# Score products of two attentions over all 128 rows of the array, and a small-tile path to memory for one attention's output

## The chip, the cores and the metric

The kernel runs on one core of one Trainium2 chip. The metric is the device time of one execution, from the first instruction to the last, in microseconds. TensorE (PE) multiplies, VectorE (DVE) and ScalarE (ACT) read the products out of PSUM, GpSimd (POOL) works between tiles in SBUF, and the queue of SyncE (SP) issues all transfers to and from memory.

## The reference

Two decoder layers run one after another on 1024 tokens of 1024 features. In each, one input projection is split into four token mixers, whose outputs go through one output projection, a layer norm, a SwiGLU feed-forward part and a second layer norm. The change lies in two of the mixers, which are both attentions with four heads:

```python
# mixer B: latent attention; keys and queries have 64 plain and 32 rotary features
q = rms_norm(c_q) @ w_uq;  kv = rms_norm(c_kv) @ w_ukv
q = concat([q[..., :64], rope(q[..., 64:])]);  k = concat([k_nope, rope(k_r)])   # k_r is shared by the heads
o = softmax(q @ k.T * 96 ** -0.5, causal) @ v
# mixer C: dilated attention; three branches with masks of their own, merged by their softmax sums
o = sum_r w_r * softmax(q @ k.T * 0.125, mask_r) @ v          # q, k rotated, 64 features
# after the mixers
x = layer_norm(alpha * x + concat([y_a, y_b, y_c, y_d]) @ w_out)
```

The three branches of mixer C have one score matrix, and the kernel folds their masks into one additive mask (`maskC`), so that both mixers run through the same routine.

## The kernel before

**Products in split form.** A float32 operand is held as a high part and a low part in float32r, and a product is taken as high x high + high x low + low x high. In the score product of one head (64 features) the stationary tile `q1[hh]` holds the head's high query part twice, on rows 0 to 63 and on rows 64 to 127, and the moving tile `kst[hh]` holds the high key part on one half of the rows and the low key part on the other. One product over 128 rows so gives high x high and high x low. The third part, low query x high key, is a product over 64 rows alone: `qlo[half]` against `kst[hh][half]`, where `half` is the 64 rows of the head (scores, line 793). Mixer B adds the rotary part as a third product, over 96 rows: `QR` has the 32 rotary features as (high, high, low), `R` as (high, low, high).

**Attention.** `attn` goes through 64 rows in each layer: four groups of 16 (mixer C heads 0 and 1, C heads 2 and 3, B heads 0 and 1, B heads 2 and 3), and in a group 2 heads x 8 query tiles of 128 tokens, a short row and a long one in turn. Row i has (i + 1) x 128 keys in pieces of at most 512. So a group has 24 score pieces, a layer 96, the kernel 192: 96 of mixer C with two products each, 96 of mixer B with three. A row goes through this chain:

- PE: the score products of a piece into a PSUM tile `sc` (L119 is the helper that issues them).
- DVE: scale, mask and running minimum of the negated scores into `P` (L798); for rows of two pieces one more instruction takes the minimum of the two (L802).
- ACT: the exponential in place with the row sum (L805). DVE: the reciprocal (L807). POOL: `P` times the reciprocal (L808).
- PE: 128x128 transposes of `P` (L825). ACT and DVE: split into `PH` and `PL` (L138, L141).
- PE: products with the values (L846). ACT: two copies of 64x256 out of PSUM into `tmp` (L853, L854). POOL: their sum (L855) into the output tile, `Yc` for mixer C and `Yb` for mixer B.

**What sets the order.** On PE the order is written by hand: scores run 3 rows ahead of the transposes, and these 2 rows ahead of the values (`AHEADS`, `VLAG`). Between them stand jobs in small pieces: the last projection tiles of mixer C (`zc`), the transposes of its queries and keys (`ptc`), and, within the second group, the projections of mixer B (`prb`, `pvb`, `ptr`, `pkb`, `pqb`). On the other engines a scheduler orders the instructions, and each engine then takes them strictly one after another. Tiles come from pools of a fixed number of buffers (A, B, E, w, t2); a tile gets a buffer when an earlier one is released.

**Around it.** `put_q` fills `q1` and `qlo` from PSUM, for half of the tokens at a time. The projections of mixer B's queries have the same form as the scores: the features 128 to 191 of the latent stand on 64 rows as high parts and on the other 64 as low parts (`Q2`); the product with the low weights is over 64 rows (`wq[1][0:64]`, lines 1005 and 1052). At the end of the second group, `end1` writes both `Yc` tiles to memory (`spill`), from where the output projection reads them back (`yr`).

Of the kernel before, what the change touches and what calls it, by code (L numbers as in the profile page):

```python
# [7 lines left out]
F32 = mybir.dt.float32  # L8
# [7 lines left out]
D = 1024  # L16
# [31 lines left out]
class Split:  # L48
    """the parts of a float32 array, each a tile of its own: [:, 0, columns] the high part, [:, 1, columns] the low one"""
# [8 lines left out]
class Net:  # L58
# [84 lines left out]
    # ---------------------------------------------------------------- consts  # L143
# [22 lines left out]
    def warm(self, n):  # L166
        """products that nothing reads, while the first operands come in: the tensor engine is slow when it starts"""
# [6 lines left out]
    def rope_tables(self):  # L174
# [27 lines left out]
        # cos(r) = sin(pi/2 - |r|)  # L202
# [7 lines left out]
    def rope(self, out, src, nh, hf, cs, sn, add_eng=None):  # L210
        """src [128, nh, 2*hf] PSUM; cs/sn [128, 2*hf]; out [128, nh, 2*hf] or with a leading copy dim."""
# [6 lines left out]
        if out is None:  # L218
            return a, b
        for o in out:  # L220
            (add_eng or nc.vector).tensor_tensor(out=o, in0=a, in1=b, op=ALU.add)
# [10 lines left out]
    def first_pair(self, T):  # L232
        """the first two k tiles of weights and tokens, one after the other, to start the products early"""
# [15 lines left out]
    def dense_tok(self, out, T, tt, W, n, c0, nn, ks=range(KD)):  # L249
        """out[128 tokens, nn] += x @ W[:, c0:c0+nn]; W units hold two k tiles of n columns."""  # L250
# [11 lines left out]
    def dense_jobs(self, name, T, tt, W, n, c0, nn, evac, step=6):  # L262
        """dense_tok as a list of steps of a few products each"""
# [24 lines left out]
    # ------------------------------------------------------------- mixer A  # L288
    def mix_a(self, l, T):
# [24 lines left out]
        # keep w[s, t] where t - s >= 0  # L314
# [28 lines left out]
        for h in range(2):  # L343
# [4 lines left out]
            if wide:  # L348
                # all token tiles of the half together, as the operands come in
# [34 lines left out]
    # ------------------------------------------------------------- mixer D  # L384
    def mix_d(self, l, T):
# [312 lines left out]
    # ------------------------------------------------------------- projections of B and C  # L698
    def z_b(self, l, T):
# [5 lines left out]
        krt = self.uw("kr", F32, "E")  # L705
        kr, junk = krt[:, 0:768].rearrange("p (t n) -> p t n", t=NT), krt[:, 768:960]
        for t in range(NT):
# [17 lines left out]
            outs = [kr[:, t, a * 32:(a + 1) * 32].unsqueeze(1) for a in range(3)]  # L725
            self.rope(outs, src, 1, 16, self.cs2[:, t, 0:64:2], self.sn2[:, t, 0:64:2])
        return ckv, cq1, cq2, kr

    def z_c(self, l, T):
        """both head pairs; the last four token tiles of the second pair are left as jobs"""  # L730
        nc, io = self.nc, self.io
        out, jobs = [], []
        for g in range(2):
# [3 lines left out]
            def evac(pz, t, q=q, k=k, v=v):  # L737
                nc.scalar.copy(v[:, t, :], pz[:, 256:384])
                src = pz[:, 0:256].rearrange("p (h j) -> p h j", j=64)
                a, b = self.rope(None, src, 4, 32, self.cs2[:, t, :], self.sn2[:, t, :])  # L740
# [12 lines left out]
    # ------------------------------------------------------------- attention  # L753
    def qk_tiles(self, pool):
        f = lambda n: self.u(n, F32R, pool)
        return [f("kst") for _ in range(2)], [f("q1") for _ in range(2)], self.u("qlo", F32R, "A")
# [8 lines left out]
    def put_q(self, pq, q1, qlo, cols):  # L765
# [925 lines left out]
```

## Time and profile before

| | us |
|---|---|
| median of 3 runs (2571.95 to 2581.69) | 2574.62 |
| span of the profiled execution | 2581.1 |
| PE busy in it | 2483.1 (96%) |
| DVE busy | 1682.5 (65%) |
| POOL busy | 1291.1 (50%) |
| ACT busy | 1039.9 (40%) |
| attention of the first layer, first score product to the output projection in steady run | 284.4 to 497.3 |
| attention of the second layer | 1573.9 to 1783.5 |

The profiled execution stands 6.5 us above the median, at the upper end of the three runs. The busy time of PE adds up the records of its products; they overlap, and a product that waits inside the array still counts as busy. How densely PE works is therefore read from the time between the starts of two products that follow each other, and not from its busy time. The granted clock (PEclk) is a share of full speed: 1.00 is 2.4 GHz, 0.50 is 1.2 GHz, and a value between them is a stretch with both.

### The profile page before, as it was taken

To read this page: it belongs to the slowest core of one execution; us is meant where nothing else is said; L and a number is where in the kernel's file an instruction comes from. 1 tells how busy PE (TensorE), PEld (TensorE's weight loads), DVE (VectorE), ACT (ScalarE), POOL (GpSimd) and SP (SyncE) were. 2 spreads that over 40 slices of the span, in tenths; PEclk is the share of its full clock that TensorE was granted. 3 is DMA by queue.
4 is the path that set the end of the run, shared out by engine and by line. 5 is a ranking of instruction groups with operands and counts; after the bars stand their busy time and mean duration, and the time that the engine had idled before them with its cause. 6 is when DMAs were issued, how large, how long until landed. Compare 5 with 4: busy or idle time off the path is not lost.

```text
span 2581.1 us, 33291 instructions
## 1 busy us (share of the span) xinstructions
PE 2483.1 (96%) x11884; PEld 2007.8 (78%) x11884; DVE 1682.5 (65%) x3132; ACT 1039.9 (40%) x2102; POOL 1291.1 (50%) x1116
## 2 busy tenths in 40 slices
PE   9999999998999999999899999999989999999997
PEld 9779767786888888778697797667868888887675
DVE  7643587458555455999966435775686554559998
ACT  6322577524323323433343225685343333234331
POOL 2014324566545454879520143245665544448795
PEclk9999999899999999999999999999999999999998
DMA  4111001331221223612131110014212222235121
GB/s 162 47 33 46 13 1 66 126 111 49 90 90 66 89 92 117 225 66 82 70 94 43 33 46 13 1 57 144 102 50 98 82 74 90 82 136 207 67 81 65
DMA packets 60822, 206.94 MB, mean 80 GB/s; under 512 B 8098, under 2 KB 8418, under 8 KB 60658
## 3 DMA queue, kind: packets, MB, share of 16 engines
q1 hardware_dynamic: 60658, 204.82, 22.8%
q8 instruction: 95, 1.56, 0.3%
q14 instruction: 69, 0.57, 0.1%
HBM read 158.62 MB, written 46.17 MB: 79 GB/s over the span
## 4 chain that ended last, share of the span: by engine, by line
PE 74%; DVE 15%; POOL 4%; issue 3%; ACT 3%; DMA 2%; POOLq 0%; DVEq 0%; SPq 0%; ACTq 0%
PE gu L119 30%; PE dn L119 5%; PE zc L119 5%; PE sc L119 5%; PE zvo L567 4%; PE po L119 4%; PE zdq L519 4%; PE za L119 3%; PE pv L846 3%; PE zb L119 2%; PE pt L825 2%; POOL dc L1254 2%; DVE ma L1467 1%; PE dl L119 1%; DMA hr<-hs 1%
## 5 line engine op out<-in xcount | busy, mean ns | idle before, releaser
L119 PE MATMUL gu<-T,fc 128*128 128x512 f32 x2640 | 636.0, 397 | 19.3 <-POOL T L1329 6.4
L119 PEld LDWEIGHTS gu<-T,fc 128*128 128x128 f32 x2640 | 499.6, 190 | 142.2 <-POOL T L1329 8.8
L1254 POOL TENSOR_TENSOR fc<-fw,fc 128x512 fp32r<-128x512 f32 x264 | 366.4, 1390 | 367.5 <-ACT fc L1253 363.5
L119 PE MATMUL dn<-dc,dc 128*128 128x512 f32 x1512 | 365.3, 402 | 21.6 <-DVE md L1518 5.4
L119 PEld LDWEIGHTS dn<-dc,dc 128*128 128x128 f32 x1512 | 287.5, 192 | 99.2 <-DVE ma L1518 8.5
L1253 ACT CAST fc<-fw 128x512 fp32r<-128x512 f32 x264 | 162.6, 620 | 373.3 <-PE gu L119 234.8
L1378 DVE TENSOR_TENSOR Ra<-Ra,gu 128x512 f32<-128x512 f32 x172 | 117.3, 684 | 225.1 <-PE gu L119 221.9
L119 PE MATMUL gu<-B,fc 128*128 128x512 f32 x1056 | 260.9, 396 | 0.0
L119 PEld LDWEIGHTS gu<-B,fc 128*128 128x128 f32 x1056 | 197.9, 188 | 47.2
L808 POOL TENSOR_SCALAR P<-P,rs 128x256 f32<-128x256 f32 (+7 forms) x128 | 95.9, 755 | 203.3 <-DVE rs L807 162.7
L1254 POOL TENSOR_TENSOR dc<-hr,dc 128x512 fp32r<-128x512 f32 x104 | 165.0, 1595 | 49.2 <-ACT dc L1253 47.6
L119 PE MATMUL po<-wh,yT 128*128 128x512 f32 x512 | 162.1, 396 | 0.0
L132 POOL TENSOR_TENSOR wl<-raw,wh 128x768 fp32r<-128x768 f32 (+2 forms) x40 | 81.6, 2046 | 116.2 <-ACT wh L127 114.9
L119 PE MATMUL zc<-wh,xT 128*128 128x384 f32 x512 | 134.8, 340 | 0.0
L1253 ACT CAST dc<-hr 128x512 fp32r<-128x512 f32 x104 | 64.6, 621 | 154.9 <-PE dn L119 50.4
L119 PEld LDWEIGHTS po<-wh,yT 128*128 128x128 f32 x512 | 95.7, 188 | 22.1
L825 PE MATMUL pt<-ident,P 128*128 128x128 f32 x576 | 94.8, 291 | 15.3 <-DVE PL L141 10.0
L1254 POOL TENSOR_TENSOR dc<-dr,dc 128x512 fp32r<-128x512 f32 x68 | 108.9, 1601 | 0.0
L805 ACT ACTIVATE P<-P,mn 128x256 f32<-128x256 f32 (+7 forms) x128 | 99.2, 776 | 15.7 <-DVE mn L802 11.9
L119 PE MATMUL dl<-wl,hl 128*128 128x512 f32 x384 | 96.0, 407 | 9.8 <-DVE mc L1518 8.4
L141 DVE TENSOR_TENSOR PL<-pt,PH 128x512 fp32r<-128x512 f32 (+3 forms) x176 | 95.2, 557 | 12.0 <-ACT PH L138 11.1
L119 PE MATMUL po<-wl,yT 128*128 128x512 f32 x256 | 100.3, 394 | 0.0
(380 smaller groups left out, 5190.2 us busy)
## 6 DMA issues: line engine op xcount, KB each, us to landing
fw<-in_wGU SPq DMA_DIRECT2D x88, 512.0 KB, 3.8
dr<-in_wD SPq DMA_DIRECT2D x44, 512.0 KB, 5.6
hr<-hs SPq DMA_DIRECT2D x44, 512.0 KB, 6.3
hs<-Ra SPq DMA_DIRECT2D x22, 512.0 KB, 2.6
hs<-Rb SPq DMA_DIRECT2D x22, 512.0 KB, 2.9
raw<-in_wO SPq DMA_DIRECT2D x16, 512.0 KB, 3.6
x<-x SPq DMA_DIRECT2D x16, 512.0 KB, 2.6
raw<-in_wC SPq DMA_DIRECT2D x16, 384.0 KB, 3.0
```

What stands on the lines that cost most here:

```text
L119: self.nc.tensor.matmul(out, lhsT=a, rhs=b, start=first and j == 0, stop=last and j == n - 1)
L132: (eng or nc.gpsimd).tensor_sub(lo[:, :n], raw[:, :n], f32(hi[:, :n]))
L141: (lo_eng or nc.vector).tensor_sub(lo, src, f32(hi))
L519: step(lambda: nc.tensor.matmul(pz, lhsT=a, rhs=b_, start=n == 0, stop=n == 23))
L567: nc.tensor.matmul(box["p"], lhsT=a, rhs=b_, start=j == 0, stop=j == 23)
L805: nc.scalar.activation(P[:, 0:nk], P[:, 0:nk], AF.Exp, scale=-1.0, bias=m, accum_out=rs[:, 0:1])
L808: nc.gpsimd.tensor_scalar(out=P[:, 0:nk], in0=P[:, 0:nk], scalar1=rs[:, 1:2], scalar2=1.0, op0=ALU.mult, op1=ALU.mult)
L825: nc.tensor.transpose(pt[:, b * 128:(b + 1) * 128], P[:, (b0 + b) * 128:(b0 + b + 1) * 128], self.ident)
L846: nc.tensor.matmul(pv[0:m, c0:256], lhsT=V[2][:, b, hh * 64:(hh + 1) * 64] if full else V[hh][:, b, :], rhs=Pt[b // 4][:, b % 4, c0:256], ...
L1253: nc.scalar.copy(dst[:, 0:512], src)
L1254: lo_eng.tensor_sub(dst[:, 512:1024], src, f32(dst[:, 0:512]))
L1378: tt = lambda o, a, b, op: v.tensor_tensor(out=o, in0=a, in1=b, op=op)
```

## The change

**Score products.** The low query part gets a tile of 128 rows for each head, `q2[hh]`: the low part on the rows of the high keys, and zeros on the other 64 rows, which `put_q` writes on POOL (a multiplication by zero, 64x512, two of them in each call; there are 8 calls in a layer). So the product is over all 128 rows of `q2[hh]` and `kst[hh]`, with the same result. The rotary tiles hold their 32 features four times instead of three: `QR` as (high, high, low, low), `R` as (high, low, high, low). The third product is then over 128 rows too, and includes low x low. The products with the low weights in mixer B's projections take all 128 rows of `wq[1]` and `Q2`.

**Dilated output.** `Yc` and `end1` are gone. Each of the eight results of a group of mixer C, 64 partitions x 256 columns, stays in a small tile of the pool t2 and is written to memory from there.

**Minimum.** The second piece of a row starts its running minimum from the first piece's result, so L802 falls away.

**Smaller things.** The rotary key of mixer B is written by one DVE instruction of four copies instead of three instructions; the scratch of its row sums is in t2; `q2` of the third group takes one buffer of pool E and one of pool B.

The core of the diff (the rest renames, removes comments and follows from these lines):

```diff
     def put_q(self, pq, q1, q2, cols):
             nc.scalar.copy(q1[hh][r, cols], pq[r, :])
-            nc.vector.tensor_sub(qlo[r, cols], pq[r, :], f32(q1[hh][r, cols]))
+            nc.vector.tensor_sub(q2[hh][r, cols], pq[r, :], f32(q1[hh][r, cols]))
             nc.scalar.copy(q1[hh][o, cols], pq[r, :])
+            nc.gpsimd.tensor_scalar(out=q2[hh][o, cols], in0=self.ident[o, 0:1].to_broadcast([64, 512]), scalar1=0.0, scalar2=None, op0=ALU.mult)
...
-                pairs = [(q1[hh][:, qs], kst[hh][:, k0:k1]), (qlo[half, qs], kst[hh][half, k0:k1])]
+                pairs = [(q1[hh][:, qs], kst[hh][:, k0:k1]), (q2[hh][:, qs], kst[hh][:, k0:k1])]
                 if R is not None:
-                    pairs.append((QR[i // 4][0:96, hh, (i % 4) * 128:(i % 4) * 128 + 128], R[0:96, k0:k1]))
+                    pairs.append((QR[i // 4][:, hh, (i % 4) * 128:(i % 4) * 128 + 128], R[:, k0:k1]))
...
                 nc.vector.tensor_tensor_reduce(out=P[:, k0:k1], in0=sp[:, 0:k1 - k0], in1=mask[:, m0:m0 + k1 - k0], scale=-scale,
-                                               scalar=3.0e38, op0=ALU.add, op1=ALU.min, accum_out=mn[:, ch:ch + 1])
-            m = mn[:, 0:1]
-            if nch == 2:
-                nc.vector.tensor_tensor(out=mn[:, 2:3], in0=mn[:, 0:1], in1=mn[:, 1:2], op=ALU.min)
-                m = mn[:, 2:3]
+                                               scalar=mn[:, ch - 1:ch] if ch else 3.0e38, op0=ALU.add, op1=ALU.min, accum_out=mn[:, ch:ch + 1])
+            m = mn[:, nch - 1:nch]
...
+            tmp = self.t2("tmp", 512)
+            y, spill = tmp[0:64, 0:256], None
+            if "Y" in G:
+                y = G["Y"][jp // 2][64 * hh:64 * hh + 64, (jp % 2) * 256:(jp % 2) * 256 + 256]
+            else:
+                l, g = G["spill"]
+                spill = self.io["ys"][l, 2, jp // 2, 64 * hh:64 * hh + 64, g * 512 + (jp % 2) * 256:g * 512 + (jp % 2) * 256 + 256]
...
+            if spill is not None:
+                nc.sync.dma_start(spill, y)
...
-                nc.tensor.transpose(pt[0:96, j * 128:(j + 1) * 128], kr[:, half * 4 + j, :], self.ident)
-            nc.scalar.copy(R[0:96, cols], pt[0:96, :])
-            nc.vector.tensor_sub(R[32:64, cols], pt[32:64, :], f32(R[32:64, cols]))
+                nc.tensor.transpose(pt[:, j * 128:(j + 1) * 128], kr[:, half * 4 + j, :], self.ident)
+            nc.scalar.copy(R[:, cols], pt)
+            for r in (slice(32, 64), slice(96, 128)):
+                nc.vector.tensor_sub(R[r, cols], pt[r, :], f32(R[r, cols]))
...
-                    (Q2[:, ts], wq[0][:, rg2]), (Q2[0:64, ts], wq[1][0:64, rg2])])
+                    (Q2[:, ts], wq[0][:, rg2]), (Q2[:, ts], wq[1][:, rg2])])
```

**What it does to the order.** PE's sequence is the same, product for product, with the new operands. On POOL the zeros are put where a `put_q` is due. The rows below are POOL's at the end of the second group of the first layer, before the change; `P` is a row on its way to the transposes, `Yc` an output tile:

```order
L808 TENSOR_SCALAR P_677_3815<-P_677_3815,rs_681_3826 128x640
L808 TENSOR_SCALAR P_684_3842<-P_684_3842,rs_687_3848 128x512
L855 TENSOR_TENSOR Yc_425_2850<-tmp_702_3899 64x256
L808 TENSOR_SCALAR P_695_3871<-P_695_3871,rs_699_3882 128x768
L808 TENSOR_SCALAR P_706_3911<-P_706_3911,rs_709_3917 128x384
```

The same place with the change (the line numbers are the changed kernel's):

```order
L805 TENSOR_SCALAR P_682_3811<-P_682_3811,rs_686_3821 128x640
L805 TENSOR_SCALAR P_689_3838<-P_689_3838,rs_692_3844 128x512
L772 TENSOR_SCALAR q2_698_3853<-ident_152 64x512 x2
L857 TENSOR_TENSOR tmp_708_3895<-tmp_708_3895 64x256
L772 TENSOR_SCALAR q2_697_3852<-ident_152 64x512 x2
L805 TENSOR_SCALAR P_701_3868<-P_701_3868,rs_705_3878 128x768
L805 TENSOR_SCALAR P_712_3908<-P_712_3908,rs_715_3914 128x384
```

Four writes of zeros (both halves of two tiles) now stand ahead of the row `P_701`, which had only one sum ahead of it.

On SP, in the first layer, the two writes of `Yc` stood behind the load of the second mask:

```order
L1073 DMA maskC_2848<-in_c_maskC 128x1024
L925 DMA gs_14459<-in_b_g 128x3
L1092 DMA maskB_4069<-in_c_maskB 128x1024
L1579 DMA ys<-Yc_2850 128x1024
L1579 DMA ys<-Yc_2851 128x1024
L124 DMA raw_5245<-in_wO 128x1024
```

With the change:

```order
L859 DMA ys<-tmp_3949 64x256
L1087 DMA maskB_4070<-in_c_maskB 128x1024
L859 DMA ys<-tmp_4057 64x256
L859 DMA ys<-tmp_4112 64x256
L859 DMA ys<-tmp_4239 64x256
L859 DMA ys<-tmp_4274 64x256
L124 DMA raw_5236<-in_wO 128x1024
```

Sixteen small writes take the place of two: twelve ahead of the mask's load and four behind it, all ahead of the output projection's weights.

## Rows read from the trace of the kernel before

**Rows 1.** Busy time by group of heads (C, C, B, B), both layers: stretch, length, busy, PEclk, DMA
```profile
core 0: us, PE busy (x) PEld busy (x) DVE busy (x) ACT busy (x) POOL busy (x), PEclk, DMA share, GB/s
284.40:328.70 44.30, 41.59 (x195) 28.79 (x194) 30.53 (x101) 30.42 (x70) 16.12 (x23) 0.88 0.00 1
328.70:388.40 59.70, 55.25 (x324) 41.24 (x321) 48.55 (x149) 42.36 (x108) 16.57 (x22) 1.00 0.01 1
388.40:434.80 46.40, 44.77 (x243) 31.92 (x241) 34.73 (x110) 37.75 (x88) 17.33 (x24) 1.00 0.17 58
434.80:497.30 62.50, 60.11 (x284) 45.02 (x282) 33.50 (x106) 41.58 (x97) 34.08 (x37) 0.78 0.20 66
1573.90:1620.60 46.70, 41.80 (x195) 29.35 (x193) 30.92 (x101) 30.85 (x70) 16.01 (x23) 0.89 0.00 1
1620.60:1683.90 63.30, 59.14 (x322) 43.71 (x321) 49.12 (x148) 42.29 (x108) 16.69 (x22) 0.92 0.00 1
1683.90:1730.40 46.50, 44.85 (x244) 32.00 (x242) 34.77 (x110) 37.82 (x88) 17.16 (x24) 1.00 0.11 37
1730.40:1783.50 53.10, 48.96 (x283) 36.31 (x282) 35.49 (x106) 40.89 (x97) 34.60 (x37) 1.00 0.27 93
```

**Rows 2.** Timeline of PE in the first group: start, duration, rows*columns, tile; 128*128 is full
```profile
318.72 0.44 PE L119 MATMUL sc<-kst,q 128*128 128x384 f32 x1
319.09 0.44 PE L119 MATMUL sc<-kst,qlo 64*128 64x384 f32 x1
319.46 0.39 PE L846 MATMUL pv<-PH,V 128*128 128x256 f32 x1
...
319.80 0.28 PE L846 MATMUL pv<-PH,V 128*128 128x256 f32 x1
319.92 0.28 PE L846 MATMUL pv<-PL,V 128*128 128x256 f32 x1
```

**Rows 3.** Timeline of PE in the third group: one score piece of mixer B
```profile
396.06 0.36 PE L119 MATMUL sc<-kst,q 128*128 128x256 f32 x1
396.35 0.38 PE L119 MATMUL sc<-kst,qlo 64*128 64x256 f32 x1
396.67 0.39 PE L119 MATMUL sc<-R,QR 96*128 96x256 f32 x1
396.89 0.86 PE L119 MATMUL pkb<-kvT,wk 128*128 128x512 f32 x3
```

**Rows 4.** Timeline of PE, queries of mixer B: products with high and low weights, and what follows
```profile
376.99 0.82 PE L119 MATMUL pqb<-cq2T,wq 128*128 128x512 f32 x2
377.74 0.38 PE L846 MATMUL pv<-PH,V 128*128 128x256 f32 x1
```

**Rows 5.** Busy time in five shorter stretches of the first layer, columns as in rows 1
```profile
294.00:300.00 6.00, 4.45 (x26) 2.85 (x24) 5.02 (x19) 4.90 (x13) 3.14 (x5) 1.00 0.00 0
300.00:309.00 9.00, 8.79 (x26) 5.66 (x27) 5.38 (x13) 5.52 (x12) 3.16 (x4) 0.50 0.01 3
357.00:378.00 21.00, 20.12 (x116) 14.70 (x115) 19.36 (x59) 16.92 (x44) 7.35 (x9) 1.00 0.01 3
378.00:399.00 21.00, 20.90 (x113) 14.91 (x112) 16.97 (x47) 19.52 (x44) 7.42 (x10) 1.00 0.07 25
444.00:471.00 27.00, 26.79 (x92) 20.34 (x91) 12.38 (x37) 15.21 (x34) 16.14 (x16) 0.51 0.23 79
```

**Rows 6.** Second layer's attention, groups of instructions by shape: count, busy us, mean ns, idle before
```profile
L802 DVE TENSOR_TENSOR mn<-mn 128x1 f32<-128x1 f32 x32 | 9.6, 301 | 0.2
L1030 DVE TENSOR_TENSOR QR<-ptr,QR 32x512 fp32r<-32x512 f32 x8 | 5.4, 688 | 1.6 <-ACT QR L1029 1.5
L808 POOL TENSOR_SCALAR P<-P,rs 128x512 f32<-128x512 f32 x7 | 4.9, 694 | 6.8 <-DVE rs L807 4.9 <-DVE mn L802 1.5 <-PE pt L825 0.2
L141 POOL TENSOR_TENSOR V<-zcv,V 128x512 fp32r<-128x512 f32 x2 | 2.5, 1276 | 2.3 <-ACT V L138 2.3
```

**Rows 7.** Transfers of the output of mixer C, median us to landing
```profile
ys<-Yc SPq DMA_DIRECT2D x4, 512.0 KB, 2.6
```

More of the change, by code (lines that the diff above doesn't have):

```diff
@@ L208, in rope_tables, with rope @@
         nc.vector.tensor_copy(self.cs2[:, :, 32:64], self.cs2[:, :, 0:32])
-    def rope(self, out, src, nh, hf, cs, sn, add_eng=None):
+    def rope(self, src, nh, hf, cs, sn):
         nc = self.nc
@@ L217, in rope @@
         nc.vector.tensor_tensor(out=b[:, :, hf:w], in0=src[:, :, 0:hf], in1=sn[:, hf:w].unsqueeze(1).to_broadcast([128, nh, hf]), op=ALU.mult)
[L218 to L221, printed above, removed]
+        return a, b
     def load_x0(self, T, h, q):
@@ L724, in z_b @@
             src = pz[:, 320:352].unsqueeze(1)
-            outs = [kr[:, t, a * 32:(a + 1) * 32].unsqueeze(1) for a in range(3)]
-            self.rope(outs, src, 1, 16, self.cs2[:, t, 0:64:2], self.sn2[:, t, 0:64:2])
+            a, b = self.rope(src, 1, 16, self.cs2[:, t, 0:64:2], self.sn2[:, t, 0:64:2])
+            nc.vector.tensor_tensor(out=kr[:, t, :].rearrange("p (a n) -> p a n", a=4), in0=a.to_broadcast([128, 4, 32]),
+                                    in1=b.to_broadcast([128, 4, 32]), op=ALU.add)
         return ckv, cq1, cq2, kr
@@ L751, in z_c, with qk_tiles @@
         return out, jobs
-    def qk_tiles(self, pool):
-        f = lambda n: self.u(n, F32R, pool)
-        return [f("kst") for _ in range(2)], [f("q1") for _ in range(2)], self.u("qlo", F32R, "A")
+    def qk_tiles(self, pool, pool2=None):
+        f = lambda n, p=pool: self.u(n, F32R, p)
+        return [f("kst") for _ in range(2)], [f("q1") for _ in range(2)], [f("q2", p) for p in (pool2 or (pool, pool))]
     def put_k(self, pk, kst, cols):
@@ L847, in values @@
                                      start=b == 0 and x == 0, stop=b == nb - 1 and x == len(pairs) - 1)
-            y = Y[jp // 2][64 * hh:64 * hh + 64, (jp % 2) * 256:(jp % 2) * 256 + 256]
+            tmp = self.t2("tmp", 512)
[5 more added lines that the diff above has]
+                spill = self.io["ys"][l, 2, jp // 2, 64 * hh:64 * hh + 64, g * 512 + (jp % 2) * 256:g * 512 + (jp % 2) * 256 + 256]
             if full:
                 nc.scalar.copy(y, pv[0:64, 0:256])
-                return
-            tmp = self.t2("tmp", 512)
-            nc.scalar.copy(tmp[0:64, 0:256], pv[0:64, 0:256])
-            nc.scalar.copy(tmp[0:64, 256:512], pv[64:128, 0:256])
-            nc.gpsimd.tensor_tensor(out=y, in0=tmp[0:64, 0:256], in1=tmp[0:64, 256:512], op=ALU.add)
-        def finish(n):
-            values(n)
-            if n % NG == NG - 1:
-                rows[n][0].get("end", lambda: None)()
+            else:
+                nc.scalar.copy(tmp[0:64, 0:256], pv[0:64, 0:256])
+                nc.scalar.copy(tmp[0:64, 256:512], pv[64:128, 0:256])
+                nc.gpsimd.tensor_tensor(out=y, in0=tmp[0:64, 0:256], in1=tmp[0:64, 256:512], op=ALU.add)
+            if spill is not None:
+                nc.sync.dma_start(spill, y)
         NG = 16
@@ L888, in attn @@
                     elif x == "v" and m >= 0 and rows[m][3] % 2 == 1:
-                        finish(m)
+                        values(m)
     def prep_c_jobs(self, zc, out):
@@ L896, in part @@
         def part(half, src):
-            kst, q1, qlo = out["qk"]
+            kst, q1, q2 = out["qk"]
             cols = slice(half * 512, half * 512 + 512)
@@ L1013, in rot @@
             for j in range(2):
-                qr = self.t2("qr", 384).rearrange("p (h a n) -> p h a n", h=4, a=3)
-                nc.vector.tensor_tensor(out=qr, in0=a[:, j].unsqueeze(2).to_broadcast([128, 4, 3, 32]), in1=b[:, j].unsqueeze(2).to_broadcast([128, 4, 3, 32]), op=ALU.add)
+                qr = self.t2("qr", 512).rearrange("p (h a n) -> p h a n", h=4, a=4)
+                nc.vector.tensor_tensor(out=qr, in0=a[:, j].unsqueeze(2).to_broadcast([128, 4, 4, 32]), in1=b[:, j].unsqueeze(2).to_broadcast([128, 4, 4, 32]), op=ALU.add)
                 qrs.append(qr)
@@ L1073, in start0 @@
             nc.sync.dma_start(m, io["c_maskC"])
-            box["Yc"] = [self.u("Yc").rearrange("p (a n) -> p a n", a=2) for _ in range(2)]
-            G[0].update(mask=m, Y=yv(box["Yc"], 0))
+            G[0].update(mask=m, spill=(l, 0))
             self.jobs = zjobs + self.prep_c_jobs(zc[1], G[1])
         def start1():
-            G[1].update(mask=G[0]["mask"], Y=yv(box["Yc"], 1))
+            G[1].update(mask=G[0]["mask"], spill=(l, 1))
             w = box["w"] = self.b_weights(l)
             def st():
-                bb["qk"] = self.qk_tiles("E")
+                bb["qk"] = self.qk_tiles("E", ("E", "B"))
             self.jobs = self.b_vqr_jobs(ct, w, bb) + [st] + self.b_qk_jobs(0, ct, w, bb, "qk")
-        def end1():
-            self.dump(f"yc{l}", box["Yc"])
-            self.spill(l, 2, box["Yc"])
         def start2():
@@ L1102, in attention @@
             g["start"] = f
-        G[1]["end"] = end1
         self.attn(G)
```

23 lines of the change are left out of this document (11 added, 12 removed).

## The prediction

> **What bounds the kernel now.** I read the page first: PE has records over 96% of the span, so the question is what PE does in the two stretches that the change touches. Then the busy time by group of heads [rows 1]. In all eight groups PE is covered by records from end to end, while the next engine stands well below: DVE leads the others in the first two groups (48.55 of 59.70 us in the second), ACT in the last two (37.75 of 46.40 in the third). So PE sets the pace, and the second engine has about 18% of air.
>
> The timeline of PE then shows what its time consists of. In the products with the values a new stationary tile comes with every product, all over 128 rows, and two products of 256 columns start 0.12 us apart [rows 2]. That is the price of 128 rows following 128 rows: 0.12 for 256 columns, 0.18 for 384, 0.24 for 512 by proportion. In the same rows the score product of 384 columns takes 0.37 until the 64-row product starts, and this one 0.37 until the next 128-row product: 0.19 too long each. In mixer B, at 256 columns, the steps are 0.29 (128 to 64 rows), 0.32 (64 to 96) and 0.22 (96 to 128) where 0.12 would do [rows 3]. PE loses about 0.1 to 0.2 us whenever a product covers another number of rows than the one before it, and a busy share doesn't show it, since the waiting product counts as busy.
>
> **What it removes on PE.** A piece of mixer C has two such changes: 0.74 against 0.36, so 0.38 us [rows 2]. A piece of mixer B has three: 0.83 against 0.36, so 0.47 us [rows 3]. There are 24 pieces in a group and 96 of each kind in both layers: 9.1 us in a group of C, 11.3 in a group of B, 36.5 + 45.1 = 81.6 in all. Two projection products of mixer B, one over 128 rows and one over 64, take 0.75 where 0.48 would do [rows 4], so 0.27 for each product with low weights. There are 12 in a layer (8 of rotary queries and 2 of plain ones in the second group, 2 more in the third): 2.7 and 0.5 us, 6.5 in all. PE could so end 88 us earlier. No product is added, and the padded ones stream the same columns.
>
> **What is late next.** PE alone would make the groups 35.2, 47.9, 34.6 and 51.2 us long in the first layer and 37.6, 51.5, 34.7 and 41.8 in the second. In the second group DVE has 48.6 and 49.1 us of work, in the third ACT has 37.8: more than PE would leave them. So the gain must be cut there. In two stretches of 21 us DVE and ACT reached 19.36 and 19.52 us, 92 and 93% [rows 5], with PE nearly covered as well; over a whole group, with its change of heads, I take 90% as what the fuller of the two can keep up. Then, length before minus length after, where the later of PE and that engine decides:
>
> - first groups, PE decides (DVE would need 30.5/0.9 = 33.9 and 34.4): 9.1 + 9.1
> - second groups, DVE decides (53.9 and 54.6): 5.8 + 8.7
> - third groups, ACT decides (41.9 and 42.0): 4.5 + 4.5
> - fourth groups: in the first layer PE decides (51.2; ACT 46.2): 11.3; in the second ACT (45.4): 7.7
>
> The sum is 60.7 us.
>
> **What it adds, and what moves.** DVE loses 32 minima of 0.30 us in a layer, 9.6 us [rows 6]. The second piece now has to wait for the first piece's result instead, which gives back between nothing and all of it. It gains two subtractions of the fourth rotary copy, 0.69 each by the 32x512 row [rows 6], and eight copies that are a third wider, under 0.2 each. Within the second group, where DVE decides, that is a quarter of the minima (2.4 us) against 3 us: I count nothing, bounds -2 and +3 us in a layer.
>
> POOL gets 16 writes of zeros in a layer. The trace has no such instruction; the nearest rows are the multiplication of 128x512, 0.69 us, and the one with float32r output, 1.28 us [rows 6]. I take the first, since it has one input like the new one. So 11 us in a layer (up to 20) on an engine with 84 us of work in some 210 [rows 1]. They come four at a time, 2.8 us ahead of a row `P` that waits for its transposes. Four places in a layer: the first under the projection of mixer C, where no score waits; three within the attention. A row's scores are taken three rows ahead, some 8 us at 2.7 us a row, so most of it is hidden; if nothing were hidden, it would be 6 x 2.8 = 17 us (31 at the higher price). I take 4 us in all.
>
> The small writes cost SP and the transfer engines nothing that anyone waits for: the large write took 2.6 us to land [rows 7], the small ones come some 6 us apart, and what stands behind them in SP's queue, mask and output weights, is wanted many rows later. A result's tile is held until it has landed, one of six of its pool at a time. If a copy out of PSUM had to wait for such a buffer, it would hold up ACT behind it; I count nothing, at most 1 us for each of 32 results. The freed `Yc` buffers bring no gain that a wait in these rows could show. On the rotary key, three DVE instructions become one, in a stretch where PE has work of its own.
>
> **Sum.** 2581.1 - 60.7 + 4 = 2524 for an execution like the profiled one. This one is 6.5 us above the median and holds 27 us at half clock in the first layer's fourth group, which the second layer's lacks: 62.5 against 53.1 us with the same work [rows 1, 5]. I take the difference to the median as such a stretch and predict 2524 - 6.5 = 2518 for the median.
>
> **Rivals.**
>
> *The other engines hold the pace that they have.* If DVE and ACT can't rise above 82%, their share in the second and third groups today, those groups give next to nothing (0.5 and 3.4, 0.4 and 0.4), the first ones 7.1 and 9.0, the fourth 11.3 and 3.2. That is 35 us: 2581 - 35 - 6.5 = 2540. For it: each engine takes its instructions strictly in order, and a row's chain crosses four engines. Against it: the 92 and 93%. Chance 0.17.
>
> *PE gets all of it.* 88 us, 2486. It would need DVE at over 100% in the second group; only if the lost minima and shorter waits inside DVE's records count more than I think. Chance 0.08.
>
> *Slower: the clock.* Before the first stretch at half clock, 294 to 300, PE had records over 4.45 of 6 us, with waits between; then the clock went to 0.50 for 9 us [rows 5]. With the change PE waits for DVE and ACT more often. One stretch of 27 us at half clock costs 9.4 us (62.5 against 53.1). From some 165 us of such stretches beyond today's, the gain of 57 is gone; with the whole attention at 1.2 GHz, 365 us, it would be 127 less today's 20 (the PEclk of the four groups below 1.00 make some 58 us at half clock [rows 1]), so 2575 - 57 + 107 = 2625. Against it: the array streams the same columns in less time, so it is idle for a smaller share than now, when it waits at each change of rows; and at half clock PE is the bound again. Chance 0.05.
>
> *The change doesn't do what it says.* The gap might belong to the score tile or to its operands, not to the number of rows, and stay: 2575. Against it, the value products change their stationary tile each time, and so do the projections, at 0.12 and 0.24. Chance 0.02.
>
> *Weight loads come out of hiding.* If the load of a stationary tile could only run beside a product on other rows, each of the 288 padded products would take the time back that it gave: 2575, no change. The value products, 0.12 apart with a new 128-row tile each, speak against it [rows 2]. Chance 0.03. The Trainium skill, "TensorE: Matmul & The Clock Gate", in Part 3 on packing small matmuls, states that a weight load overlaps products in flight only when their row groups differ, which would lead here; the trace doesn't agree, by the same 0.12 us.
>
> **How the numbers follow.** Forecast 2518, chance 0.65, own range 2500 to 2535 (DVE and ACT at 88 to 95%, zeros hidden or not). With the first rival, whose own zeros and waits may add some us, the range goes up to 2550; below I leave out all but the edge of the second, 2492. That leaves 0.08 below and 0.10 above. Faster by over 0.5% (which is about what a measurement of this kernel can tell from no change): 0.65 + 0.17 + 0.08 = 0.90. Within 0.5%: 0.05. Slower: 0.05.
>
> **What would show it.** In the timeline of PE after: the three score products of mixer B 0.12 us apart at 256 columns and some 0.22 to 0.24 at 512, and no 64- or 96-row form left. By group: third groups at about 42 us with ACT near 90%, second at about 54 with DVE near 90%; PE with real gaps there, ended by `PL`, `P` or `mn`. If the third group is at 35, PE got it all; if at 46 with ACT at 82%, the chain across the engines is the bound. Stretches at half clock should be no longer than now; were they to fill the attention, the rival of the clock holds. Zeros that are not hidden would show as PE waiting for POOL's `P` in the rows behind them. I am wrong if the steps within the triple stay above 0.2 at 256 columns, or if the copies into `tmp` wait for transfers.

## The result

The kernel with the change took 2538.8 us in the median of four runs (2535.17 to 2540.48), the kernel before beside it 2577.55: a ratio of 0.9845, 95% interval 0.9821 to 0.9869. That is faster by 1.5% and 21 us above the forecast of 2518. It is inside the range, but above the forecast's own part of it (2500 to 2535), in the part that was added for the first rival. The profiled execution of after has a span of 2535.7 us against 2581.1, 45.4 less.

The steps on PE are what the forecast said for the padded products. Timeline of PE, third group of after, one and a half score pieces of mixer B (answers [rows 3]; x2 is the products with the high and the low query part):

```profile
403.70 0.40 PE L119 MATMUL sc<-kst,q 128*128 128x512 f32 x1
403.94 0.39 PE L119 MATMUL sc<-R,QR 128*128 128x512 f32 x1
404.17 0.52 PE L119 MATMUL sc<-kst,q 128*128 128x384 f32 x2
404.52 0.34 PE L119 MATMUL sc<-R,QR 128*128 128x384 f32 x1
404.70 0.38 PE L822 MATMUL pt<-ident,P 128*128 128x128 f32 x2
```

From start to start 0.24 and 0.23 us at 512 columns; at 384 columns 0.35 for two and 0.18 for the third. In before a 64-row product of 384 columns took 0.37 [rows 2]. No 64- or 96-row product is left among the scores.

Busy time by group of after, cut at PE's first score product of a group (columns and cuts as in [rows 1]; the last rows are mixer B's second pair of heads):

```profile
core 0: us, PE busy (x) PEld busy (x) DVE busy (x) ACT busy (x) POOL busy (x), PEclk, DMA share, GB/s
284.40:322.70 38.30, 31.46 (x194) 25.92 (x194) 30.23 (x93) 30.23 (x71) 21.69 (x26) 0.96 0.03 8
322.70:384.50 61.80, 48.95 (x324) 41.34 (x322) 51.41 (x144) 43.17 (x108) 25.90 (x27) 0.94 0.06 16
384.50:426.80 42.30, 38.04 (x241) 32.77 (x241) 32.89 (x98) 37.15 (x88) 22.94 (x28) 0.96 0.11 36
426.80:473.60 46.80, 40.58 (x283) 35.54 (x282) 32.12 (x101) 40.34 (x97) 34.09 (x36) 1.00 0.26 86
1550.30:1587.80 37.50, 31.94 (x196) 26.30 (x194) 30.15 (x92) 30.10 (x71) 21.68 (x26) 0.95 0.03 8
1587.80:1651.30 63.50, 51.62 (x322) 44.35 (x320) 51.69 (x145) 43.93 (x109) 25.10 (x27) 0.87 0.07 18
1651.30:1692.90 41.60, 37.82 (x241) 32.94 (x241) 32.22 (x97) 36.31 (x87) 22.76 (x27) 0.96 0.04 8
1692.90:1739.80 46.90, 40.56 (x283) 35.52 (x281) 32.12 (x101) 40.44 (x97) 34.11 (x36) 1.00 0.31 105
```

| group | forecast gain, L1 + L2 | measured gain, L1 + L2 |
|---|---|---|
| first (C) | 9.1 + 9.1 | 6.0 + 9.2 |
| second (C, and mixer B's projections) | 5.8 + 8.7 | -2.1 - 0.2 |
| third (B) | 4.5 + 4.5 | 4.1 + 4.9 |
| fourth (B) | 11.3 + 7.7 | 15.7 + 6.2 |
| sum | 60.7 | 43.8 |

So 17 us are missing, and nearly all of it in the two second groups: PE has 6 to 8 us less busy time there and they are no shorter. (4 of the 17 were allowed for as the cost of the zeros, and 1.6 us were gained outside of these groups, so the span is 11 us off.) What PE waits for in the first layer's second group of after (waiting product <- what released it: us, times, longest):

```profile
PE ptr L1026 <- DVE qr L1015: 6.1, 6, 2.2
PE sc L119 <- DVE mn L798: 3.3, 3, 2.2
PE pt L822 <- DVE QR L1030: 1.5, 1, 1.5
```

All three are waits for DVE: `qr` is the sum that forms the rotary queries in four copies, `mn` the running minimum, `QR` the low rotary parts. DVE is busy over 51.41 of 61.80 us there, 83%, not 90. The experiments ask why.

### The profile page after: what moved, and what is told of

It is laid out like the page before. It is cut to its first block, busy times and chain, and to the rows that moved or that the text cites. A ratio compares the mean times of both kernels' runs of the same rounds, so it can differ in the third digit from the quotient of the medians.

```text
span 2535.7 us, 33381 instructions
## 1 busy us (share of the span) xinstructions
PE 2405.2 (95%) x11884; PEld 1993.6 (79%) x11884; DVE 1674.2 (66%) x3040; ACT 1038.7 (41%) x2102; POOL 1347.0 (53%) x1148
## 5 line engine op out<-in xcount | busy, mean ns | idle before, releaser
L119 PEld LDWEIGHTS gu<-B,fc 128*128 128x128 f32 x1056 | 197.8, 188 | 46.9
L1247 ACT CAST dc<-hr 128x512 fp32r<-128x512 f32 x104 | 64.6, 621 | 150.7 <-PE dn L119 47.0
L119 PE MATMUL sc<-kst,q 128*128 128x512 f32 (+3 forms) x384 | 110.9, 384 | 13.6 <-DVE mn L798 13.5
L802 ACT ACTIVATE P<-P,mn 128x256 f32<-128x256 f32 (+7 forms) x128 | 99.5, 779 | 27.0 <-DVE mn L798 25.4
```

The lines of the kernel that those rows point to most:

```text
L119: self.nc.tensor.matmul(out, lhsT=a, rhs=b, start=first and j == 0, stop=last and j == n - 1)
L802: nc.scalar.activation(P[:, 0:nk], P[:, 0:nk], AF.Exp, scale=-1.0, bias=m, accum_out=rs[:, 0:1])
L1247: nc.scalar.copy(dst[:, 0:512], src)
```

## The experiments

All lengths below are cut at DVE's first mask instruction of a group and of the next, for all kernels alike, so they differ by a few us from those above. They come from one profiled execution of each kernel. L1 / L2 are the two layers. Each ratio is to the kernel before as run beside that experiment, whose medians there were 2578.48 to 2582.68 us.

| kernel | median, us | ratio to before, 95% | first groups | second groups | DVE busy in them | third groups |
|---|---|---|---|---|---|---|
| before | 2577.55 | | 44.5 / 46.9 | 62.2 / 65.7 | 50.4 / 51.0 | 44.1 / 44.3 |
| after | 2538.8 | 0.9845 (0.9821 to 0.9869) | 38.7 / 37.8 | 64.4 / 64.8 | 53.5 / 53.0 | 39.6 / 40.3 |
| scores over 64 and 96 rows | 2585.41 | 1.0024 (1.0006 to 1.0041) | 47.9 / 49.1 | 67.0 / 65.9 | 54.6 / 53.7 | 49.4 / 44.5 |
| output path alone | 2577.8 | 0.9984 (0.9966 to 1.0002) | 41.1 / 46.0 | 63.1 / 64.2 | 49.7 / 50.4 | 45.7 / 45.7 |
| value splits grouped | 2535.61 | 0.983 (0.9805 to 0.9855) | 37.7 / 37.7 | 63.4 / 65.8 | 53.4 / 53.5 | 38.2 / 39.6 |
| all splits grouped | 2535.53 | 0.9826 (0.9803 to 0.9849) | 38.1 / 39.6 | 62.7 / 62.4 | 53.2 / 52.7 | 39.2 / 39.1 |
| rotary sum on POOL | 2539.96 | 0.9849 (0.9821 to 0.9878) | 38.6 / 37.0 | 64.6 / 64.6 | 48.8 / 48.9 | 39.7 / 38.2 |
| both of these | 2542.34 | 0.9861 (0.9842 to 0.9879) | 36.5 / 39.9 | 65.0 / 65.2 | 48.2 / 47.7 | 38.4 / 39.2 |
| rotary product over 96 rows | 2537.5 | 0.9838 (0.9815 to 0.9861) | 37.6 / 38.7 | 62.5 / 62.5 | 53.4 / 52.7 | 38.3 / 40.3 |
| rotary part as before | 2529.74 | 0.9793 (0.9761 to 0.9825) | 37.6 / 37.9 | 59.6 / 59.5 | 50.3 / 50.0 | 38.9 / 40.3 |
| zeros twice | 2558.36 | 0.9913 (0.9894 to 0.9931) | 42.2 / 40.6 | 65.3 / 66.5 | 54.0 / 53.6 | 43.6 / 43.2 |
| zeros by a fill | 2539.31 | 0.9826 (0.9786 to 0.9866) | 36.6 / 36.7 | 62.2 / 62.4 | 52.5 / 52.6 | 43.0 / 42.9 |
| rotary as before, fill, grouped | 2534.8 | 0.9814 (0.9779 to 0.9848) | 37.9 / 39.0 | 58.7 / 58.7 | 49.7 / 49.8 | 40.0 / 38.9 |
| rotary as before, values paired | 2531.46 | 0.9821 (0.9789 to 0.9854) | 37.6 / 37.5 | 59.4 / 59.4 | 50.4 / 50.4 | 37.4 / 38.8 |

### Is it the number of rows?

The change, with the score products back on 64 and 96 rows of the same tiles:

```diff
-pairs = [(q1[hh][:, qs], kst[hh][:, k0:k1]), (q2[hh][:, qs], kst[hh][:, k0:k1])]
+pairs = [(q1[hh][:, qs], kst[hh][:, k0:k1]), (q2[hh][half, qs], kst[hh][half, k0:k1])]
-    pairs.append((QR[i // 4][:, hh, ...], R[:, k0:k1]))
+    pairs.append((QR[i // 4][0:96, hh, ...], R[0:96, k0:k1]))
```

> The changed kernel, but the score products read 64 rows (low query part) and 96 rows (rotary part) of the same tiles again; zeros, small output tiles, one minimum less and all else of the change stay. Theory of the change of rows: the steps on PE go back to 0.3 to 0.4 us, so the first, third and fourth groups lose the 6 to 9, 4 to 5 and 6 us that they gained, and the time comes back to 2565 to 2585. Rival (the gain is in the lighter DVE work, the freed buffers or the output path): it stays within 10 us of 2539.

The gain is gone, ratio 1.0024. Timeline of PE in its third group, one and a half pieces:

```profile
406.26 0.90 PE L119 MATMUL sc<-kst,q 128*128 128x512 f32 x2
407.09 0.50 PE L119 MATMUL sc<-R,QR 96*128 96x512 f32 x1
407.43 0.82 PE L119 MATMUL sc<-kst,q 128*128 128x512 f32 x2
408.18 0.50 PE L119 MATMUL sc<-R,QR 96*128 96x512 f32 x1
```

The form shown for an x2 is that of its first product. 0.83 and 0.75 for the pair and 0.34 for the rotary product, where after has 0.24 each. The whole gain comes from the rows of the score products, and what else came with the change costs about 6 us by the ratio (its interval allows 2 to 11). This run takes back the 64 and the 96 rows together; which of them counts is shown further down, where the 96 rows come back alone.

### The output path alone

Before, with the small output tiles and their writes (`y = tmp[0:64, 0:256]` and a transfer for each, as in the diff ahead).

> The kernel before, with the small output tiles alone. Theory of the change of rows: no change, 2570 to 2585, all groups as before. Rival (the freed buffers carry part of the gain): 2550 to 2565. Rival (a tile that waits for its transfer holds up ACT in the second group): slower, 2585 to 2595, and the second group longer by 3 to 5 us in a layer.

No difference, 0.9984 with 1 inside the interval. In after the small writes land in this time (count, size, median us):

```profile
ys<-tmp SPq DMA_DIRECT2D x32, 64.0 KB, 1.9
```

### Do copies and subtractions that alternate between ACT and DVE hold up the second group?

A helper splits each value tile by an ACT copy and a DVE subtraction, one pair after another. First the four copies and then the four subtractions; and the same for keys and queries too:

```diff
-                for hh in range(2):
-                    self.split(V[g][hh][...0:64], V[g][hh][...64:128], pv[...])
+            for hi, lo, src in parts:
+                nc.scalar.copy(hi, src)
+            for hi, lo, src in parts:
+                nc.vector.tensor_sub(lo, src, f32(hi))
```

> The changed kernel; the four value splits of a job are written as four copies on ACT and then four subtractions on DVE, instead of in turn. Theory of the alternation (in the second group ACT stood 5.9 us waiting for DVE between value copies out of one PSUM tile, and PE behind both): those waits go, the second groups get 4 to 8 us shorter each, time 2524 to 2532. Rival (DVE has as much work as the second group can hold, 51.4 of 61.8 us): the waits move elsewhere, time 2535 to 2543.

> As the run before, and the splits of queries and keys in the same way (all copies on ACT first, then DVE). Theory of the alternation: another 1 to 4 us in the second and third groups, 2520 to 2530. Rival (DVE's work): 2535 to 2543, no difference to the run before beyond 3 us.

The value splits alone leave the second groups where they were (63.4 / 65.8), with all splits they are 2 us shorter, which is no more than two executions of one order can differ by (below). As a main cause it falls: some 8 us a layer are to be explained, and the medians lie 3 us below after's, with overlapping intervals.

### Is it DVE's work, and which?

The sum that writes the four rotary copies of the queries, moved to POOL, alone and together with all grouped splits:

```diff
-nc.vector.tensor_tensor(out=qr, in0=a..., in1=b..., op=ALU.add)
+nc.gpsimd.tensor_tensor(out=qr, in0=a..., in1=b..., op=ALU.add)
```

> The changed kernel, with the eight additions that write the rotary queries (5.1 us of DVE in the second group) on POOL. Theory that DVE's work bounds the second group (53.5 of 64.4 us, 2.9 to 3.0 of 3 us in its first third): both second groups get 3 to 6 us shorter, 2527 to 2533. Rival (the chain from engine to engine sets its length, whatever DVE has to do): the second groups stay within 1.5 us, 2536 to 2542, and a POOL that is in the way of the rows would make them longer.

> The same with all splits grouped (copies on ACT first, then subtractions on DVE). Theory of DVE's work: 2520 to 2530, second groups at 57 to 60 us. Rival: 2532 to 2538 as with grouping alone.

DVE lost 4 to 5 us of work in the group and the group got no shorter. POOL's rows in the first layer's second group of the first of them, and what PE waited for:

```profile
L1015 POOL TENSOR_TENSOR qr<-ra 128x512 f32<-128x512 f32 x8 | 10.0, 1273 | 11.1 <-DVE ra L1011 6.5 <-DVE rs L804 4.6
L772 POOL TENSOR_SCALAR q<-ident 64x512 fp32r<-64x512 f32 x4 | 5.9, 1485 | 0.1
```

```profile
PE ptr L1026 <- POOL qr L1015: 6.9, 6, 2.1
PE sc L119 <- DVE mn L798: 3.3, 3, 2.2
```

POOL takes 1273 ns where DVE took 684, after waits for DVE, and PE waits for the same tile, now from POOL. This moved the work without taking it from the chain to `ptr`, so it doesn't tell the amount of DVE's work from the length of that chain.

Two more undo the rotary padding. In one only the product is back on 96 rows, the four copies stay; in the other three copies are made and 96 rows read, as before. The second block shows the two places that change DVE's work in the second group; the transposes, ACT's copies and the score product go back to 96 rows with them, and the key's copies are three, still by one instruction.

```diff
-    pairs.append((QR[i // 4][:, hh, ...], R[:, k0:k1]))
+    pairs.append((QR[i // 4][0:96, hh, ...], R[0:96, k0:k1]))
```

```diff
-            for r in (slice(32, 64), slice(96, 128)):
+            for r in (slice(32, 64),):
                 nc.vector.tensor_sub(R[r, cols], pt[r, :], f32(R[r, cols]))
-                qr = self.t2("qr", 512).rearrange("p (h a n) -> p h a n", h=4, a=4)
+                qr = self.t2("qr", 384).rearrange("p (h a n) -> p h a n", h=4, a=3)
```

> The changed kernel, but the rotary score product reads 96 rows of the same tiles again; only PE changes. Two changes of rows come back in each of 96 pieces, some 0.1 to 0.2 us each: 7 us in a third or fourth group on PE. Theory that ACT bounds these groups (37 of 42 us): PE had about 7 us of air there, so most of it is hidden, 2540 to 2548. Rival (PE sets the pace there): 2560 to 2568.

> The changed kernel with the rotary part as it was before: three copies, 96 rows, tiles and all. It takes 2.4 us of work from DVE in the second group of each layer and gives two changes of rows for each of 96 pieces back to PE. Theory that DVE's own work bounds the second group: second groups 2 to 3 us shorter, fourth groups as in the run with 96 rows alone, 2530 to 2536. Rival (the chain across the engines bounds it): 2536 to 2542.

The product over 96 rows costs nothing that can be measured (0.9838 against 0.9845), and the timeline of PE shows why. It was expected that two late starts would come back in each piece, and they did not. The first three lines are of the kernel with 96 rows, third group; the last two are of before, first group, right behind a 64-row product, and the second of them is one that [rows 2] leaves out:

```profile
403.36 0.40 PE L119 MATMUL sc<-R,QR 96*128 96x512 f32 x1
403.60 0.63 PE L119 MATMUL sc<-kst,q 128*128 128x512 f32 x2
404.07 0.39 PE L119 MATMUL sc<-R,QR 96*128 96x512 f32 x1
```

```profile
319.46 0.39 PE L846 MATMUL pv<-PH,V 128*128 128x256 f32 x1
319.68 0.28 PE L846 MATMUL pv<-PL,V 128*128 128x256 f32 x1
```

From the product over 96 rows to the next over 128 it is 0.24 us at 512 columns, and the pair behind it takes 0.47 until the next product over 96: the same pace as among products over 128 rows. Over all 48 of these products the median step is 0.23 us into one from 128 rows, where in before, from the 64-row product, it was 0.43. The last two lines show a step of 0.22 us in mixer C of before, between two products of 128 rows and 256 columns, where later ones take 0.12 [rows 2]: the second product behind a 64-row one starts 0.1 late too. So the late starts belong to the 64-row product and to the two products behind it. In before the 96-row product stood right there, and its steps of 0.22 us at 256 columns [rows 3] and 0.34 at 512 looked like its own. Among the scores the padded queries carry the whole gain on PE, and the fourth rotary copy gains nothing there.

In this kernel every engine takes the same instructions in the same order as in after, apart from the 96 rows. Still its second groups are 2 us shorter, so 2 us is what two executions of one order can differ by. The granted clock goes with it. The start of the second layer's second group up to the same place, 34 DVE instructions, in after and in the kernel with 96 rows (columns as in [rows 1]):

```profile
1588.50:1603.40 14.90, 11.59 (x70) 10.22 (x70) 10.89 (x34) 8.84 (x25) 5.10 (x6) 0.79 0.04 10
1585.60:1598.40 12.80, 9.49 (x72) 8.43 (x71) 10.87 (x34) 8.79 (x25) 5.05 (x6) 1.00 0.05 12
```

DVE has the same work in both, and the stretch is 2.1 us longer where 0.79 of the clock was granted.

Taking the copies away as well shortens both second groups by 3 us more than this, to 59.6 and 59.5. One pair of profiles would not settle that against the 2 us, but it repeats: in the three kernels with the rotary part as before these groups take 58.7 to 59.6 us, and with the scores over 128 rows or with the 96 alone, and four copies by DVE, 62.2 to 66.5. DVE's rows in the first layer's second group, of after (first two) and of the kernel with the rotary part as before:

```profile
L1015 DVE TENSOR_TENSOR qr<-ra 128x512 f32<-128x512 f32 x8 | 5.1, 684 | 0.0
L975 DVE TENSOR_TENSOR R<-ptb,R 32x512 fp32r<-32x512 f32 x4 | 2.8, 691 | 0.1
```

```profile
L1015 DVE TENSOR_TENSOR qr<-ra 128x384 f32<-128x384 f32 x8 | 4.1, 548 | 0.0
L975 DVE TENSOR_TENSOR R<-ptb,R 32x512 fp32r<-32x512 f32 x2 | 1.4, 684 | 0.1
```

That is 2.4 us of work (5.1 + 2.8 against 4.1 + 1.4). Over the whole group DVE has 53.4 / 52.7 us with the copies and 50.3 / 50.0 without (both with 96-row products), and the groups are 2.9 and 3.0 shorter. That the copies cost this is shown; whether by the amount of DVE's work or by the longer way to `ptr` and `QR` is not, since both went at once. The busy time by group of the kernel with the rotary part as before, and of after, both at this section's cut:

```profile
322.70:382.30 59.60, 49.44 (x329) 42.42 (x329) 50.29 (x146) 44.69 (x113) 24.98 (x28) 0.94 0.07 19
1585.20:1644.70 59.50, 48.06 (x329) 40.81 (x328) 50.02 (x145) 44.60 (x113) 24.89 (x28) 0.97 0.07 19
```

```profile
323.50:387.90 64.40, 51.00 (x336) 42.92 (x335) 53.48 (x149) 45.70 (x114) 26.21 (x28) 0.95 0.07 17
1588.50:1653.30 64.80, 52.88 (x329) 45.48 (x329) 53.02 (x148) 45.15 (x113) 25.47 (x28) 0.87 0.07 17
```

DVE is busy over 84% of these groups in the one, 82 and 83% in the other. In all kernels without 64-row products and with the rotary sum on DVE it is 81 to 85%.

### What do the zeros cost?

Written twice, and written by a fill in place of the multiplication:

```diff
+            nc.gpsimd.tensor_scalar(out=q2[hh][o, cols], in0=self.ident[o, 0:1].to_broadcast([64, 512]), scalar1=0.0, scalar2=None, op0=ALU.mult)
```

```diff
-            nc.gpsimd.tensor_scalar(out=q2[hh][o, cols], ..., scalar1=0.0, scalar2=None, op0=ALU.mult)
+            nc.gpsimd.memset(f32(q2[hh][o, cols]), 0.0)
```

> The changed kernel with every write of zeros done twice, 16 more of them on POOL in a layer. Theory that they are hidden but for some us: 2540 to 2546. Rival (POOL's writes hold up the rows behind them, and the change pays for that): as much again as the first 16 cost, 2550 to 2562, with PE waiting for POOL's rows.

> The changed kernel, with the zeros written by a plain fill on POOL in the same places, instead of a multiplication, which took 1.49 us. What a fill of 64x512 takes there isn't known; well under 1 us is likely. Theory that the zeros cost what they hold up (16 more in a layer cost 17 us in all): 2522 to 2532, the first and third groups 2 to 3 us shorter each. Rival (the first 16 of a layer were hidden, only the doubled ones stood in the way): 2535 to 2542.

The durations of one write of zeros (min, median, max ns), of after and of the kernel with the fill:

```profile
L772 POOL TENSOR_SCALAR q<-ident x32: 1479/1486/1502, 269.5 to 1661.8; 64x512 fp32r<-64x512 f32 x32
```

```profile
L772 POOL MEMSET q<- x32: 517/521/525, 269.8 to 1658.5; 64x512 f32 x32
```

Twice as many cost 18 us by the ratios (20 by the medians) for 47.6 us more of POOL's time, some two fifths of it, mostly in the first and third groups (3.5 / 2.8 and 4.0 / 2.9). The fill saves 31 us of POOL's time and gains nothing: the first groups get 2.1 / 1.1 us shorter and the second 2.2 / 2.4, the third get 3.4 / 2.6 longer and the fourth 1.3 each. What the zeros cost as they stand these runs don't tell, because the scheduler's order changed with their length; two thirds of their time taken away gained nothing that can be measured.

### Further relief

On the kernel with the rotary part as before: first fill and grouped splits added, then, in their place, the values of both heads in one tile, so that one copy and one subtraction split both (`self.split(t[:, :, :, 0:64], t[:, :, :, 64:128], pv...)` in place of two).

> Both of these together with the grouped splits (copies on ACT first, then subtractions on DVE). If the parts add: 2515 to 2525. If the second group's chain takes everything up again: 2525 to 2533, no better than the fill alone.

> The rotary-undone kernel once more, with one more relief of VectorE: the two heads' value rows of a key tile lie side by side in one tile, so that one ScalarE copy and one VectorE subtraction of double width split both (in the second groups 8 copies and 8 subtractions fewer, by the mean lengths of those rows about 1.2 us less VectorE work and 1 us less ScalarE work per layer). Theory that VectorE's work sets the second groups: each of them is 1 to 3 us shorter than in the rotary-undone kernel (59.6), so 2522 to 2528 us. Rival that the chain from engine to engine sets them, not the amount of VectorE work: the second groups stay at 59 to 60 us, so 2527 to 2533 us.

Neither is faster than the rotary part as before (2534.8 and 2531.46 against 2529.74, intervals overlapping). The first has second groups of 58.7, and its first groups take that back. In the second, DVE's work in the second groups did not fall as meant: it is 50.4 / 50.4, since splits of the next group's keys moved in; the groups stayed, at 85%. So it tested neither theory. It does show that the clock is not what holds DVE there: in its second layer the group ran at full clock to the end, with DVE at 85% (columns as above):

```profile
1582.50:1641.90 59.40, 49.02 (x341) 41.54 (x341) 50.43 (x138) 45.25 (x107) 24.17 (x28) 1.00 0.08 20
```

Second and third group together did get shorter, 96.8 / 98.2 against 98.5 / 99.8, and the profiled span is 4 us shorter (2526.3 against 2530.5), which the medians don't bear out.

The lowest median is that of the kernel with padded query tiles and the rotary part as before: 0.9793 against the kernel before. It is 5 us below after by the profiled spans and 9 by the medians, which were not taken side by side; the two intervals still overlap at their edges.

## Why the prediction was right, and where it was off

**Late starts around products of fewer rows: right in size, and too general.** Steps of 0.24, 0.23 and 0.18 us, as worked out from the value products; with the rows put back, all of the gain is gone. But the prediction put the loss down to every change in the number of rows, and read the 0.22 us behind the 96-row product as a change from 96 to 128. With 96 rows between 128 and 128 nothing is lost (0.23 and 0.24 us at 512 columns). The cause is the 64-row product and reaches two products behind it, so the sum of 0.47 us for a piece of mixer B stands, and padding the queries alone gives it back. The rival that the gap stays and the one of weight loads are out: the products above have three different stationary tiles of 128 rows. The Trainium skill, "TensorE: Matmul & The Clock Gate", Part 3 on packing small matmuls, states that a weight load overlaps products in flight only when the row groups differ; these starts do not agree with that line, though the same Part makes an exception for loads into the background weight buffer, which no run here shows.

**Who is late next: right in kind, and in size for four groups of eight.** The six groups other than the second ones were to give 46.2 us and gave 46.1. That the sums agree so well is luck, since the first layer's first and fourth groups are off by 3 and 4 us in opposite directions. The third groups are 42.3 and 41.6 long with ACT at 88 and 87% (forecast 41.9 and 42.0 at 90%; the rival that PE gets all had 34.6 and 34.7). The first layer's first group fell 3.1 us short, where PE waits 2.2 us for `mn`, 1.6 for POOL's `P` and 1.4 for `PL`, each in one or two places. Its fourth gave 4.4 more, because the stretch at half clock is not there in this execution: PEclk went from 0.78 [rows 1] to 1.00.

**The second groups: two terms were mis-sized.** They were to give 14.5 us and gave -2.3. The parts below add up to this by DVE's busy share, which is a sum and not a test; some of it is the clock of this execution, since with the same order on every engine the kernel with 96 rows has second groups 1.9 and 2.3 us shorter.

- *90% for DVE.* Measured, it is 83 and 81% (51.41 of 61.80, 51.69 of 63.50). With the 48.55 and 49.12 us of before [rows 1] and 82%, the groups would be 59.2 and 59.9, a gain of 0.5 and 3.4 in place of 5.8 and 8.7: 10.6 us of the error. This is the first rival's number, and in these two groups DVE did stay at the share that the rival gave it; in the third groups ACT did not. The 92% that I took for evidence held over 21 us [rows 5], not over 60.
- *Added against removed work on DVE, "I count nothing".* The fourth copy adds 2.4 us in the group, near the 3 that I had. But the minima that it was set against were shorter there than the mean over the attention [rows 6], and the chained minimum costs time of its own. DVE's rows in the second group of before, and in after:

```profile
L802 DVE TENSOR_TENSOR mn<-mn 128x1 f32<-128x1 f32 x8 | 1.5, 189 | 0.1
```

```profile
L798 DVE CUSTOM_DVE_ANT_0 P<-sc,maskC 128x512 f32<-128x512 f32 x10 | 6.8, 683 | 0.1
L798 DVE CUSTOM_DVE_ANT_0 P<-sc,maskC,mn 128x512 f32<-128x512 f32 x2 | 1.5, 748 | 0.1
```

So 1.5 us go and some 0.5 come back (8 pieces by about 0.06), and the balance is +1.4 us and not 0. DVE's whole busy time in the group rose by 2.9 and 2.6 (51.41 and 51.69 against [rows 1]), the rest being work that fell to the other side of the cut. At 82% that is 3.5 and 3.1 us, about the 6.2 of the error that are left. The kernel with the rotary part as before bears it out: without these copies the second groups are 3 us shorter.

**What stays open** is why DVE doesn't get beyond 81 to 85% there. ACT's copies, the chain to `ptr`, and PE's waits in turn may all be in it, and no run tells them apart; with the splits grouped it stayed in these bounds, and with the rotary sum on POOL it fell to 76%. The clock goes with some 2 us between executions (0.87 granted in the second layer of after, 0.92 in the kernel with 96 rows), but not the bound, since a group at full clock reached 85% as well.

**The first rival's total: near by luck.** It gave 2540, and 2538.8 was measured. But it has 35 us from the groups where 43.8 came, and its step to the median, the same 6.5 us, failed as the forecast's did.

**The zeros: the price was wrong, the total is open.** 1.49 us each, outside of both neighbours (0.69 and 1.28, [rows 6]), so 24 us of POOL's time in a layer and not 11. PE waits for POOL's `P` once in the first layer's first group, 1.6 us, the sign that was named for zeros that are not hidden. The 4 us that I counted are neither confirmed nor refuted by the two experiments.

**The output path and the clock: right.** The small writes alone change nothing that can be measured, and none of ACT's copies into `tmp` waits for a transfer in after's attention. The mean granted clock of after is 0.980, no attention group lies below 0.87, and by the PEclk of the groups some 37 us ran at half clock where it was 58.

**The step to the median: wrong.** I took 6.5 us off for a stretch at half clock. In after the profiled execution lacks that stretch, and the median stands 3.1 us above its span, so this step is 9.6 us of the 21; the other 11.3 lie in the span (2524.4 against 2535.7).

## What to carry to other kernels

Read PE's pace from starts of products that follow each other: a busy share of 96% hid 0.1 to 0.2 us at each of three starts around every 64-row product, and padding it with zeros to 128 rows gave them back, but the time fell only in the stretches where PE was the last to finish. Before padding, look at each operand on its own: the padded queries carry the gain, while the 96-row product lost nothing among products of 128 rows. Its fourth copy cost VectorE 2.4 us a layer in the group where VectorE has the most work, and without it that group is some 3 us shorter. A late step can belong to the product before the last one, so change one operand at a time. Before a difference of 2 us between groups of single profiles is explained, compare two kernels with the same order, and their clock. For the engine that becomes the next bound, take the share that it reached over a stretch as long as the one you forecast, not its best 21 us. In after it was 81 to 83% on VectorE over the second groups and 87 to 88% on ScalarE over the third, where 92 and 93% had been seen over 21 us.

## What the runs showed of the hardware

- A product over 64 rows among products over 128 and 96 rows made three starts late, by 0.1 to 0.2 us each: its own and those of the two products behind it. A product over 96 rows between products over 128 made none late (0.23 and 0.24 us from start to start at 512 columns).
- A multiplication by zero of 64x512 into float32r took GpSimd 1.49 us, a fill of the same tile as float32 0.52 us, although the multiplication of a 128x512 float32 row takes 0.69 [rows 6].
- A mask-and-minimum on VectorE that starts from another instruction's minimum takes 748 ns in place of 683 at 128x512; the separate minimum that it replaces took 189 in the first layer's second group (301 over the second layer's attention [rows 6]).
- The rotary sum of 128x512 takes 684 ns on VectorE and 1273 on GpSimd.
